# A two-layer attention step on one core: both attentions rewritten from "item after item" to a pipeline in beats

## The chip, the core and the metric

One core of a Trainium2 chip runs the whole program. Five engines work from queues of their own: TensorE (PE, with its weight loads listed as PEld), VectorE (DVE), ScalarE (ACT), GpSimd (POOL), and SyncE (SP), which here only issues DMAs. Each engine takes its instructions in the order in which they stand in its queue, and an instruction that waits holds up everything behind it on that engine. The metric is the device time of one execution in microseconds (us): the median of three runs before is 3446.29 us (3445.15 to 3455.32).

## The reference

2048 prompt frames and 64 sample frames of width 1024 (16 heads of 64) pass through two layers, all in float32:

```
# layer 0 (mixer A)
q, k, v, gate = split(rms_norm(x) @ w_in_a, 4)
s = q @ k.T * 0.125 + rel_bias;  masked to the own chunk of 64 frames and the 8 chunks before it
x = x + ((softmax(s) @ v) * silu(gate)) @ w_out_a
# shared keys and values, from the new x
k, v = split(rms_norm(x) @ w_kv, 2)
# layer 1 (mixer B), strictly causal, over all frames (the sample: 2048 cached frames and its own)
q, gate = split(rms_norm(x) @ w_in_b, 2)
z = q @ k.T * 0.125
w = exp(log_sigmoid(z) + sum over later keys of log_sigmoid(-z))      # stick breaking
x = x + ((w @ v) * silu(gate)) @ w_out_b
y = rms_norm(x)
```

The new k and v rows of both layers are outputs too.

## The kernel before

**Precision.** A float32 operand x is kept as two parts, hi = copy of x in the PE's float32 format and lo = x - hi (`split`: ACT writes hi at L136, DVE subtracts at L137). A projection then takes three matmuls instead of one (L155 to L157).

**Stages.** Four stages follow one another: projections of layer 0, attention A ("band"), projections of layer 1, attention B ("sticks"). Projections go through DRAM: q, k, v and gate are stored per pair of heads (`hp`, 8 pairs) and loaded again by the attentions. The q/k/gate projections of the second half of the frames are partly put off (`DEFER`): k of head pairs 6 and 7 in A, gate and q of all pairs in B. They are done during the attention, as its filler.

**Attention.** Queries are taken in groups of 512 (g = 0 to 3), in the order of `ORDER`: part (1, 0), then part (3, 2); within a part by head pair, then group, then head h. An item of B is one (hp, g, h, c): 4 query tiles of 128 against key chunk c of 512, c from g down to 0. For each tile the PE makes scores z (L465), ACT takes the sigmoid f (L1006), POOL multiplies neighbouring pairs (`two`, L1017), DVE scans the running product over the pairs (L1019; whole rows at L1009 on the diagonal), and POOL fills in the elements between (L1022). The scan starts from the carry of the chunk c+1. An item of A is one (hp, g, h): per tile scores over 640 keys, DVE adds the bias and finds the minimum (L821), ACT takes exp (L826), DVE the reciprocal (L828), POOL scales (L829).

`weigh` then transposes the weights in blocks of up to 4 x 128 columns into a PSUM bank `wt` (PE, L128), splits them into `ph` and `pl` (L136, L137) and multiplies both with v into the bank `acc` (L497). Because B works with differences of neighbouring v rows, each tile of B also needs the last value of its diagonal: a matmul with `last_values` and the selector `upto` adds it (L507; L545 for the sample). `gate_out` sums the two halves of `acc` (ACT L475, DVE L476), multiplies by the gate (POOL L478) and stores.

**The order of the work.** `pipelined` walks through the items with a lag of one item: the four tiles of an item are written out one by one, and behind each one or two of the `weigh` blocks of the item in front, transposes, split and products of a block together. After a block a step of the filler may follow, at a rate worked out for the part. Filler are, in this order: the put-off projections (`ps_j`, L599 to L601; 6 matmuls a step, the weights of a job cut in one step of 8 ACT and 8 DVE instructions), the cut of the output weights (`w_out_steps`: each row's load is followed at once by its split, through the buffers `gt` that the gates use too), two pauses of 10 and 2 steps, and the output projections of the part that is done (`ps_o`, L690 to L692). What is left runs behind the last matmul of the attention (`tc.issue_after`). `LEAD` steps of filler (8 in A, 12 in B) run ahead of the first item.

What the code writes out is not yet the order on the engines: the program is built with `schedule_with_timeline_sim=True`, and a planner hands out the instructions in the order in which its own model of the times finds them ready, what was written first going first. The order of each queue is fixed by this before the program runs.

**Buffers** that matter: z has 2 PSUM banks; `wt` has 3 in A and 4 in B and is also used by the filler's sums; `acc` has 1; `ph` and `pl` 4 each; f 3; the passed rows `s` 9 in A and 11 in B; key and value chunks 4 each in B.

Of the kernel before, what the change touches and what calls it, by code (L numbers as in the profile page):

```python
# [9 lines left out]
F32 = mybir.dt.float32  # L10
# [6 lines left out]
P = 128  # L17
D = 1024
NK = D // P
H = 16  # L20
# [23 lines left out]
LEAD = dict(a=8, b=12)  # L44
LATER = dict(a=(100, 100), b=(150, 0))
# [22 lines left out]

@with_exitstack
def encoder_step(ctx: ExitStack, tc: tile.TileContext, a: dict, o: dict):  # L70
    nc = tc.nc
    mm = nc.tensor.matmul
# [16 lines left out]
    nc.vector.tensor_copy(identr, ident)  # L89
    nhalf = cpool.tile([P, 1], F32, name="nhalf")  # L90
    nc.gpsimd.memset(nhalf, -0.5)
# [20 lines left out]
    vend = dram.tile([len(TOK), H, P], F32R, name="v_end")  # L112

# [13 lines left out]
    def flip(out, in_):  # L127
        nc.tensor.transpose(out, in_, ident[: in_.shape[0], : in_.shape[0]])  # L128

    banks = {}  # L130
    done_late = set()
    last_mm = [None]


    def split(hi, lo, src):
        nc.scalar.activation(hi, src, AF.Copy)  # L136
        nc.vector.tensor_tensor(lo, src, f32(hi), ALU.subtract)  # L137

    def scaled_split(hi, lo, src, g):
        for k in range(NK):  # L140
            nc.scalar.activation(hi[:, k], src[:, k], AF.Copy, scale=g[:, k : k + 1])
            nc.vector.scalar_tensor_tensor(lo[:, k], src[:, k], g[:, k : k + 1], f32(hi[:, k]), ALU.mult, ALU.subtract)

    def rstd_of(pool, xt, n, junk):
        ss = pool.tile([P, 1], F32, name="ss", tag="ss", bufs=4)
        nc.scalar.activation(junk[:n], xt[:n], AF.Square, accum_out=ss[:n])
        ms = pool.tile([P, 1], F32, name="ms", tag="ms", bufs=4)
        nc.vector.tensor_scalar(ms[:n], ss[:n], 1.0 / D, EPS, ALU.mult, ALU.add)
        r = pool.tile([P, 1], F32, name="rstd", tag="rstd", bufs=4)
        nc.gpsimd.tensor_tensor(r[:n], ms[:n], nhalf[:n], ALU.pow)  # L150
# [14 lines left out]
    def projections(L, x_of, begin, w_v, cv, gv, out_v, jobs, first, prompt, sample, stages):  # L165
        with (
# [7 lines left out]
            with tc.tile_pool(name=f"v_{L}", bufs=2) as pool:  # L174

                def normed(t, scale=nc.gpsimd.tensor_scalar):
# [12 lines left out]
                order = [t for gs_ in ORDER for g in gs_ for t in range(4 * g, 4 * g + 4)] + [len(TOK) - 1]  # L189
                if L == "a":  # L190
                    order.sort()
                normed(order[0], nc.vector.tensor_scalar)
                begin()
                for half in range(2):
                    wh, wl = [], []
                    for k in range(NK):
# [5 lines left out]
                        nc.scalar.activation(h_, raw, AF.Copy, scale=gv[:, k : k + 1])  # L202
                        nc.vector.scalar_tensor_tensor(
# [4 lines left out]
                    for i, t in enumerate(order):  # L208
                        r0, n = TOK[t]
                        if half == 0 and i + 1 < len(TOK):  # L210
                            normed(order[i + 1])
# [19 lines left out]
                        if dst is not None:  # L231
                            vn = pool.tile([P, CH], F32, name="vn", tag="vn", bufs=2)
                            nc.scalar.activation(vn[:n], ps[:n], AF.Copy)
# [6 lines left out]
            with tc.tile_pool(name=f"st_{L}", bufs=5) as spool, tc.tile_pool(name=f"t_{L}", bufs=2) as pool:  # L240
                for j, (kind, w, c0, g) in enumerate(jobs):
                    for hp in range(HP):
# [10 lines left out]
                        for hf, (r0, n, chunks) in enumerate(HALVES):  # L253
# [9 lines left out]
                            for c, m in chunks:  # L263
# [8 lines left out]
                                if kind == "g":  # L272
                                    nc.scalar.activation(sg[:, c : c + m], ps[:, :m], AF.Silu)
# [7 lines left out]
                            if kind == "k":  # L281

                                cols = slice(hp * P, hp * P + P)
                                for c in range(0, HALF, CH):
                                    b = hf * HALF + c - first
                                    if b >= 0:
                                        kf = pool.tile([P, CH], F32, name="kf", tag="kf", bufs=2)
                                        part = slice(c, c + CH)
                                        nc.gpsimd.tensor_tensor(kf, f32(sh[:, part]), f32(sl[:, part]), ALU.add)
                                        natural(pool, psum, kf, 0, P, 4, prompt[b : b + CH, cols])  # L290
                                if hf == 0:
                                    kf = pool.tile([P, CH], F32, name="kf", tag="kf", bufs=2)
                                    part = slice(NEW, NEW + NS)
                                    nc.gpsimd.tensor_tensor(kf[:, :NS], f32(sh[:, part]), f32(sl[:, part]), ALU.add)
# [31 lines left out]
    def stage_diff(where, t, half, pool, psum):  # L326
# [5 lines left out]
        if where == "cache":  # L332
# [3 lines left out]
            else:  # L336
                nc.gpsimd.memset(prev, 0.0)
# [10 lines left out]
        nc.gpsimd.tensor_tensor(prev[:n], prev[:n], cur[:n], ALU.subtract)  # L348
# [4 lines left out]

    def stage_ends(half, pool, psum):
        cols, heads, n = slice(half * CH, half * CH + CH), slice(half * 8, half * 8 + 8), len(TOK)
        cur = pool.tile([P, CH], F32, name="vcur", tag="vr", bufs=2)
        nc.sync.dma_start(cur[: n - 1], vraw[1 : 1 + NP, cols].rearrange("(t p) c -> t p c", p=P)[:, P - 1])
        nc.sync.dma_start(cur[n - 1 : n], vraw[T : T + 1, cols])
        vs = pool.tile([P, 8, 2, DH], F32R, name="vs", tag="vs", bufs=2)
        split(vs[:n, :, 0, :], vs[:n, :, 1, :], cur[:n].rearrange("p (h d) -> p h d", d=DH))  # L360
        nc.sync.dma_start(f32(vend[:, heads]), f32(vs[:n]).rearrange("p h s d -> p h (s d)"))
# [799 lines left out]
```

## Time and profile before

| | |
|---|---|
| median of 3 runs | 3446.29 us |
| the profiled execution | 3465.09 us |
| its span, first to last instruction | 3463.4 us |
| granted TensorE clock in it, mean | 0.986 |
| PE busy | 3315.4 us |
| DVE busy | 1937.2 us |
| ACT busy | 1666.5 us |
| POOL busy | 1176.1 us |

The profile's page gives busy time for each engine and for the costliest groups of instructions; other views of the trace give the same for chosen stretches, the waits (who waited for whom), and the chain of work that ended last. The end of a matmul is modelled in it, and matmuls overlap in the rows: the durations of a group of matmuls can add up to more than the time that they took.

### The profile page before, as it was taken

To read this page: it belongs to the slowest core of one execution; us is meant where nothing else is said; L and a number is where in the kernel's file an instruction comes from. 1 tells how busy PE (TensorE), PEld (TensorE's weight loads), DVE (VectorE), ACT (ScalarE), POOL (GpSimd) and SP (SyncE) were. 2 spreads that over 40 slices of the span, in tenths; PEclk is the share of its full clock that TensorE was granted. 3 is DMA by queue.
4 is the path that set the end of the run, shared out by engine and by line. 5 is a ranking of instruction groups with operands and counts; after the bars stand their busy time and mean duration, and the time that the engine had idled before them with its cause. 6 is when DMAs were issued, how large, how long until landed. Compare 5 with 4: busy or idle time off the path is not lost.

```text
span 3463.4 us, 53601 instructions
## 1 busy us (share of the span) xinstructions
PE 3315.4 (96%) x18064; PEld 2829.5 (82%) x18064; DVE 1937.2 (56%) x3863; ACT 1666.5 (48%) x3609; POOL 1176.1 (34%) x1845
## 2 busy tenths in 40 slices
PE   8999999998988999999999998999999999999999
PEld 6789999987877998787899997777777776777777
DVE  3224431127888874221244336777877788777763
ACT  4223322237877773141244335555655566655641
POOL 2002210004443431020233004333466676666650
PEclk9999999999999999999999999999999999999999
DMA  6359983258898974443699568665543465434433
GB/s 187 131 191 367 342 290 132 101 180 235 239 250 239 244 201 158 130 153 107 212 347 347 193 204 223 166 178 160 165 112 98 127 179 144 109 113 135 123 99 112
DMA packets 455776, 642.52 MB, mean 186 GB/s; under 512 B 50009, under 2 KB 269177, under 8 KB 455485
## 3 DMA queue, kind: packets, MB, share of 16 engines
q1 hardware_dynamic: 396046, 587.98, 55.2%
q10 hardware_dynamic: 59456, 51.13, 4.6%
q8 instruction: 143, 2.34, 0.3%
q14 instruction: 131, 1.07, 0.1%
HBM read 387.94 MB, written 251.04 MB: 184 GB/s over the span
## 4 chain that ended last, share of the span: by engine, by line
PE 75%; DVE 10%; DMA 6%; ACT 3%; issue 3%; POOL 1%; SPq 0%; ACTq 0%; DVEq 0%; POOLq 0%
PE ps_t L156 8%; PE ps_t L155 8%; PE ps_t L157 8%; PE acc L497 8%; PE z L465 6%; PE wt L128 6%; PE ps_v L157 4%; PE ps_v L156 4%; PE ps_v L155 4%; PE ps_o L690 3%; PE ps_o L691 3%; PE ps_o L692 3%; DVE pl L137 3%; DVE s L1009 2%; DVE s L1019 2%
## 5 line engine op out<-in xcount | busy, mean ns | idle before, releaser
L128 PE MATMUL wt<-ident,s 128*128 128x128 f32 (+1 forms) x3472 | 561.5, 278 | 34.5 <-DVE pp L137 8.4
L137 DVE TENSOR_TENSOR pl<-wt,ph 128x512 fp32r<-128x512 f32 (+1 forms) x864 | 539.6, 653 | 75.4 <-ACT ph L136 73.2
L128 PEld LDWEIGHTS wt<-ident,s 128*128 128x128 f32 (+1 forms) x3472 | 425.2, 142 | 126.8 <-DVE pl L137 12.8
L136 ACT ACTIVATE ph<-wt 128x512 fp32r<-128x512 f32 (+1 forms) x864 | 464.0, 583 | 128.9 <-PE wt L128 112.1
L1006 ACT ACTIVATE f<-z 128x512 f32<-128x512 f32 (+4 forms) x680 | 354.0, 543 | 312.5 <-PE z L465 156.2
L1022 POOL TENSOR_TENSOR s<-f,s 128x256 f32<-128x256 f32 x416 | 364.8, 878 | 168.4 <-DVE s L1019 162.1
L465 PE MATMUL z<-kt,q 128*128 128x512 f32 (+3 forms) x1280 | 390.2, 400 | 22.9 <-ACT f L1006 13.1
L497 PE MATMUL acc<-pl,vt 128*128 128x512 f32 (+3 forms) x1088 | 370.4, 374 | 33.8 <-DVE pl L137 32.3
L155 PE MATMUL ps_t<-x_own,wh 128*128 128x362 f32 (+1 forms) x1152 | 378.6, 329 | 0.0
L157 PE MATMUL ps_t<-x_own,wl 128*128 128x362 f32 (+1 forms) x1152 | 377.9, 328 | 0.0
L156 PE MATMUL ps_t<-x_own,wh 128*128 128x362 f32 (+1 forms) x1152 | 377.4, 328 | 0.0
L829 POOL TENSOR_SCALAR s<-s,rc 128x640 f32<-128x640 f32 (+5 forms) x264 | 194.5, 744 | 538.3 <-DMA gt<-gate_a 282.8
L497 PE MATMUL acc<-ph,vt 128*128 128x512 f32 (+3 forms) x1088 | 359.2, 364 | 6.2 <-ACT ph L136 3.3
L1019 DVE TENSOR_TENSOR_SCAN s<-two,s,own 128x256 f32<-128x256 f32 x384 | 279.5, 738 | 75.2 <-POOL two L1017 73.7
L1017 POOL TENSOR_TENSOR two<-f 128x256 f32<-128x256 f32 x416 | 259.1, 628 | 125.2 <-ACT f L1006 124.2
L497 PEld LDWEIGHTS acc<-pl,vt 128*128 128x128 f32 x1088 | 196.0, 192 | 83.1 <-DVE pl L137 66.4
L465 PEld LDWEIGHTS z<-kt,q 128*128 128x128 f32 x1280 | 206.3, 194 | 56.5 <-ACT f L1006 32.5
L137 DVE TENSOR_TENSOR sl<-ps_t,sh 128x362 fp32r<-128x362 f32 (+2 forms) x140 | 81.1, 582 | 302.7 <-ACT sh L136 286.6
L497 PEld LDWEIGHTS acc<-ph,vt 128*128 128x128 f32 x1088 | 204.5, 192 | 42.9 <-ACT ph L136 14.6
L1009 DVE TENSOR_TENSOR_SCAN s<-f,own 128x128 f32<-128x128 f32 (+4 forms) x264 | 201.6, 789 | 47.0 <-ACT f L1006 46.0
L156 PEld LDWEIGHTS ps_t<-x_own,wh 128*128 128x128 f32 x1152 | 217.0, 188 | 0.8
L155 PEld LDWEIGHTS ps_t<-x_own,wh 128*128 128x128 f32 x1152 | 216.9, 188 | 0.8
(155 smaller groups left out, 6534.7 us busy)
## 6 DMA issues: line engine op xcount, KB each, us to landing
vt<-v_b SPq DMA_DIRECT2D x80, 512.0 KB, 5.4
v_b<-vs SPq DMA_DIRECT2D x64, 512.0 KB, 6.1
q<-q_a SPq DMA_DIRECT2D x128, 256.0 KB, 4.9
q<-q_b SPq DMA_DIRECT2D x128, 256.0 KB, 4.7
vt<-v_a SPq DMA_DIRECT2D x48, 512.0 KB, 7.5
kt<-k_b SPq DMA_DIRECT2D x96, 256.0 KB, 6.6
keys<-k_a SPq DMA_DIRECT2D x80, 256.0 KB, 6.4
v_a<-vs ACTq DMA_DIRECT2D x32, 512.0 KB, 2.8
```

What stands on the lines that cost most here:

```text
L128: nc.tensor.transpose(out, in_, ident[: in_.shape[0], : in_.shape[0]])
L136: nc.scalar.activation(hi, src, AF.Copy)
L137: nc.vector.tensor_tensor(lo, src, f32(hi), ALU.subtract)
L155: mm(out, sh(k), mh(k), start=(k == 0), stop=False)
L156: mm(out, sh(k), ml(k), start=False, stop=False)
L157: mm(out, sl(k), mh(k), start=False, stop=(k == NK - 1))
L465: mm(z, q[:, i, t * P : t * P + P], kt[:, h], start=(i == 0), stop=(stop and i == 1), skip_group_check=not stop,)
L497: last_mm[0] = mm(acc[:, c0 : c0 + m], v, part[:, at : at + m], start=(first and s == 0 and i == 0), stop=(last and s == 1 and i == len(bl ...
L1006: nc.scalar.activation(f[:, x0:], z, AF.Sigmoid, scale=-SCALE)
L1009: nc.vector.tensor_tensor_scan(pr[:, rev], f[:, rev], own[:, rev], 1.0 if carry_in is None else carry_in, ALU.mult, ALU.max if diag else A ...
L1019: nc.vector.tensor_tensor_scan(pr[:, CH - 2 :: -2], two[:, ::-1], own[:, : CH // 2], carry_in, ALU.mult, ALU.bypass)
L1022: nc.gpsimd.tensor_tensor(pr[:, 1:CH:2], by2[:, :, 1], pr[:, 2 : CH + 1 : 2], ALU.mult)
```

## The change

The diff has 1419 lines. Its parts:

1. **Beats.** `pipelined` is replaced by the class `Beat`. A beat writes out: the next step of each tile that is under way, one step of each list of small leftovers, then scores of one new tile and transposes with split of the blocks that are due (in A the scores first, in B the transposes first), then the products of blocks that were transposed at least `HOLD` beats before (1 in A, 2 in B), then filler. The first block of an item of four tiles is transposed `LAG` beats behind its last tile (2 in A, 5 in B). So a tile of B is spread over four beats: scores and sigmoid; pairs; scan; elements between.
2. **Filler as jobs** of (steps ahead, products, steps behind). The load of a job is issued at the first product of the job in front; its cuts are written in pieces of 2 rows (put-off projections) or halves (output tiles) over the second half of that job's products. Rows of the output weights are loaded three ahead, whole (512 KB instead of 2 x 256 KB), into the buffers `oh` and `ol`; a row counts as half a step. Filler is paced by a fixed number of steps a beat (`RATE`: 0.4 in A, 0.3 in B). Output tiles of a group join the filler when that group's last products are out (`when_summed`). `LEAD` is 8 in both. The rest runs at the end, without `issue_after`.
3. **Last values of B.** The matmuls L507 and L545, `last_values`, `upto`, their preparation and `stage_ends` are gone. One filler job (`end_values`) loads the 17 rows, transposes them with 8 PE transposes and keeps them as a small table; POOL adds them to `ot` in front of the gate.
4. **Sum of the halves in A.** ACT copies both halves of `acc` out (two instructions instead of one) and POOL adds them; before, DVE added. In B and for the sample DVE still adds.
5. **Loads.** Keys are loaded ahead of values, the gate only at the first block of the last item that needs it.
6. **Banks and buffers.** B: `wt` 3 instead of 4, `acc` 2 instead of 1, `ph` and `pl` 5 instead of 4, f 4 instead of 3; the row buffer `s` is taken at the scan instead of at the scores.

A wrapper `InOrder` could pin instructions to the order in which they are written; its switch `on` is set to False throughout, so it does nothing.

```diff
-LEAD = dict(a=8, b=12)
-LATER = dict(a=(100, 100), b=(150, 0))
+RATE = dict(a=0.4, b=0.3)
+LAG = dict(a=2, b=5)
+LEAD = dict(a=8, b=8)
+HOLD = dict(a=1, b=2)
...
-    def gate_out(L, pool, acc, h, c0, n, gt, ot, hp, g):
+    def gate_steps(L, pool, acc, h, c0, n, gt, sums, hp, g):
...
+        def shift():
+            if "ot" not in sums:
+                sums["ot"] = pool.tile([P, CH], F32, name="ot", tag="ot", bufs=2)
+            sums[h] = pool.tile([P, CH], F32, name="otmp", tag="otmp", bufs=1)
+            act.activation(sums[h][mine, :n], acc()[other, c0 : c0 + n], AF.Copy)
+            if L == "a" and n > NS:
+                act.activation(sums["ot"][mine, :n], acc()[mine, c0 : c0 + n], AF.Copy)
+        def close():
+            ot, tmp = sums["ot"], sums.pop(h)
+            if L == "a" and n > NS:
+                gps.tensor_tensor(ot[mine, :n], ot[mine, :n], tmp[mine, :n], ALU.add)
+            else:
+                dve.tensor_tensor(ot[mine, :n], acc()[mine, c0 : c0 + n], tmp[mine, :n], ALU.add)
+            if h == 0:
+                return
+            if L == "b":
+                t0, m = g * (CH // P), max(n // P, 1)
+                by = ot[:, :n].rearrange("p (t q) -> p t q", t=m)
+                last = ends["b"][:, hp, t0 : t0 + m].unsqueeze(2).to_broadcast([P, m, n // m])
+                gps.tensor_tensor(by, by, last, ALU.add)
+            gps.tensor_tensor(ot[:, :n], ot[:, :n], gt()[:, :n], ALU.mult)
             nc.sync.dma_start(lay[L]["o"][g][hp], ot[:, :n])
...
-            if ends and s == 0:
-                mm(acc, *ends, start=False, stop=False, skip_group_check=True)
...
+        def cut(k0):
+            ks = slice(k0, k0 + STEP)
+            scaled_split(st["wh"][:, ks], st["wl"][:, ks], st["raw"][:, ks], g[:, ks])
...
+    def w_out_steps(src, w):
+        def load(k):
+            if k < NK:
+                tag = ("oh", "ol")[k % 2]
+                raws[k] = opool.tile([P, D], F32, name="woraw", tag=tag, bufs=2)
+                nc.sync.dma_start(raws[k], src[k * P : (k + 1) * P])
...
+            ([partial(load, i) for i in range(3)] if k == 0 else [], [None], [[partial(cut, k), partial(load, k + 3)]])
...
+    class Beat:
...
+        def beat(self, first=None):
+            for tile in list(self.tiles):
+                tile.pop(0)()
+            self.tiles = [t for t in self.tiles if t]
+            self.one_rest()
...
+            while self.blocks and self.blocks[0][0] <= self.clock:
+                due.append(self.blocks.pop(0)[1:])
...
+            if first and self.scores_first:
+                self.tiles.append(first())
+            if due:
+                turn()
+            if first and not self.scores_first:
+                self.tiles.append(first())
+            self.products()
+            while due:
+                turn()
+            self.clock += 1
+            self.due = min(self.due + self.rate, 2.0)
+            while (self.now or self.beside) and self.due >= 1.0:
+                cost = self.step()
+                if not cost:
+                    break
+                self.due -= cost
+        def item(self, firsts, blocks):
+            for i, block in enumerate(blocks):
+                self.blocks.append((self.clock + len(firsts) - 1 + self.lag + i * len(firsts) // len(blocks), *block))
+            for first in firsts:
+                self.beat(first)
...
-        banks.update(wt=4, fo="wt")
+        banks.update(wt=3, fo="wt", ph=5)
...
+            def pairs():
+                gps.tensor_tensor(two, by2[:, :, 0], by2[:, :, 1], ALU.mult)
+            def scan():
+                to, carry = pr(), carry_in()
...
+            def between():
+                to, carry = st
+                gps.tensor_copy(to[:, CH : CH + 1], carry)
+                gps.tensor_tensor(to[:, 1:CH:2], by2[:, :, 1], to[:, 2 : CH + 1 : 2], ALU.mult)
...
+            return [pairs, scan, between]
...
+        def acc_bank():
+            return psum.tile([P, CH], F32, name="acc", tag="acc", bufs=2)
```

793 lines of the change are left out of this document (430 added, 363 removed).

## The prediction

> **What bounds the kernel now.** I read the page first, then busy time by stage, then the waits of the two attentions, then the chain of work that ended last, and only then single groups.
>
> ```profile
> PE 3315.4 (96%) x18064; PEld 2829.5 (82%) x18064; DVE 1937.2 (56%) x3863; ACT 1666.5 (48%) x3609; POOL 1176.1 (34%) x1845
> ```
>
> By this line the PE is full and nothing is to be won. The stages say otherwise. The columns are: stretch, its length, then busy time (and instructions) of PE, PEld, DVE, ACT and POOL, granted clock, DMA share, GB/s. The five stretches are projections of layer 0, attention A with the first output tiles, the rest of A's output with the projections of layer 1, attention B, and the output tiles behind B.
>
> ```profile
> 0.00:757.00 757.00, 743.06 (x3833) 656.92 (x3834) 226.90 (x499) 230.68 (x513) 83.30 (x89) 1.00 0.61 211
> 757.00:1342.00 585.00, 545.07 (x3450) 486.10 (x3449) 461.39 (x1240) 431.40 (x970) 242.23 (x310) 0.96 0.83 229
> 1342.00:2093.00 751.00, 742.49 (x3898) 655.97 (x3897) 220.13 (x418) 231.13 (x502) 126.10 (x142) 1.00 0.62 212
> 2093.00:3342.00 1249.00, 1172.86 (x6372) 940.91 (x6371) 981.92 (x1638) 745.99 (x1581) 709.62 (x1283) 0.98 0.50 141
> 3342.00:3463.40 121.40, 111.89 (x518) 89.57 (x516) 46.88 (x71) 27.26 (x47) 14.88 (x22) 0.99 0.34 112
> ```
>
> In the projections the PE is busy 98 to 99%; the change does not touch them, nor the output tiles at the end. What can move lies in A (585 us) and B (1249 us). There the PE shows 39.9 and 76.1 us of idle time, and DVE is at 79% in both (461.4/585 and 981.9/1249).
>
> PE busy hides short stalls, because matmuls overlap in the rows. In a stretch that is nothing but 512-column output matmuls, one starts every 40/178 = 0.225 us, while the row of such a matmul lasts 0.39 us:
>
> ```profile
> 1342.00:1382.00 40.00, 40.00 (x178) 33.13 (x177) 15.21 (x18) 8.18 (x10) 1.69 (x2) 1.00 0.59 190
> ...
> L691 PE MATMUL ps_o<-big,oh 128*128 128x512 f32 (+1 forms) x544 | 214.5, 394 | 0.0
> ```
>
> So after each matmul some 0.17 us of standstill still counts as busy, and the 76 us in B are a lower bound of the PE's loss. The Trainium skill (Perfetto Trace Analysis, Identifying the Most-Contended Engine) states the same of matmul busy time and takes the share of weight loads as the measure. The trace agrees: PEld has 656.0/751 = 87% in the third stage and 940.9/1249 = 75% in B. By that rule B at 87% would take 1077 us; by PE busy it could not go below 1173.
>
> What the PE waits for in B (waiter, releaser, us in total, times, longest):
>
> ```profile
> PEld acc L497 <- DVE pl L137: 61.5, 101, 2.0
> DVE ot L476 <- ACT otmp L475: 55.5, 27, 4.3
> ACT f L1006 <- POOL s L1022: 55.0, 55, 3.3
> ...
> PEld z L465 <- ACT f L1006: 32.5, 74, 5.9
> ...
> PEld wt L128 <- POOL s L1022: 11.8, 20, 1.2
> ...
> PEld acc L497 <- ACT ph L136: 11.1, 44, 1.1
> ACT big L136 <- DMA woraw<-in_w_out_b: 10.8, 10, 3.1
> ```
>
> Many short waits, none of them for an engine that is full: products stand right behind the split of their own block, and scores wait for a z bank whose sigmoid is late. In A there are in addition a few long ones, in the stretch without PE filler around the output weights (950 to 1100 us):
>
> ```profile
> ACT big L136 <- DMA woraw<-in_w_out_a: 18.3, 8, 6.9
> PEld z L465 <- DVE mn L821: 18.1, 14, 8.3
> ...
> ACT oh L136 <- DMA og<-o_a: 8.4, 1, 8.4
> ```
>
> ACT waits up to 6.9 us for a row of weights loaded a moment before; exp and splits queue behind it on ACT, and the PE behind those.
>
> **The change part by part.** Everything is summed against the profiled execution (3465.09 us, span 3463.4); the median of the runs is 18.8 us lower, and I subtract the differences from it. A measurement of this kernel tells about 0.3% (10 us) from no change.
>
> *Output weights loaded three rows ahead, output tiles one job ahead.* In A this takes away the ACT waits of 18.3 and 8.4 us: **-27 us**. That the chain runs through them speaks for taking them whole (shares of A's 585 us, 4.5% is 26 us):
>
> ```profile
> by line: PE acc L497 17.6%; PE wt L128 14.8%; PE z L465 14.7%; issue 4.6%; DMA woraw<-in_w_out_a 4.5%; DMA vt<-v_a 4.3%; DVE pl L137 4.0%; DVE s L821 3.9%; PE ps_o L690 3.4%; PE ps_o L691 3.2%; PE ps_o L692 3.1%; DMA q<-q_a 2.6%; PE acc L53
> ```
>
> The next thing late there is a v load (4.3%, 25 us) that the change only reorders, so I take no more. B's 10.8 us are inside B's term.
>
> *Last values.* 64 matmuls go, and 16 short ones:
>
> ```profile
> L507 PE MATMUL acc<-upto,last_values 128*128 128x512 f32 x64 | 25.6, 400 | 0.0
> L478 POOL TENSOR_TENSOR ot<-ot,gt 128x512 f32<-128x512 f32 x64 | 82.6, 1290 | 143.7 <-DVE ot L476 126.3 <-DMA gt<-gate_a 17.4
> ```
>
> At the pitch of 0.225 us that is 14.4 us of PE. Instead POOL adds over 128x512, once for each head pair and group of B: 32 x 1.29 (the nearest row, L478) = 41 us more on POOL, which is idle 539 of B's 1249 us. The ends: free, or +41 if each one holds up the pairs (L1017) behind it on POOL and with them a scan; I take 0, since scans run beats ahead of their transposes. The new job's 8 transposes and two loads are one filler step.
>
> *Halves summed in A.* For 64 (hp, g, h) DVE loses an addition, ACT gains a copy, POOL gains an addition:
>
> ```profile
> L476 DVE TENSOR_TENSOR ot<-acc,otmp 64x512 f32<-64x512 f32 x128 | 87.7, 685 | 67.3 <-ACT otmp L475 65.5
> L475 ACT ACTIVATE otmp<-acc 64x512 f32<-64x512 f32 x128 | 76.0, 593 | 79.9 <-PE acc L497 77.2
> ```
>
> DVE -44, ACT +38, POOL up to +83 us. A then holds ACT 469, DVE 418, POOL 325 of 558 us. ACT at 84% becomes A's fullest engine; at its best stretch (44.31 of 50 us, quoted below) it reaches 89%, so A could not end below 469/0.886 = 530. Inside 558 I take 0 for this part; between -28 and +38 it could be anything.
>
> *Beats in B.* The four steps of a tile stand a beat apart, transposes 5 beats behind, products 2 beats behind their split; cuts of filler weights come in pieces of 2 instead of 8 pairs. The number of beats follows from the tiles; two stretches show how full DVE and ACT can get when something else does not hold them up:
>
> ```profile
> L1006 ACT ACTIVATE f<-z 128x512 f32<-128x512 f32 (+4 forms) x680 | 354.0, 543 | 312.5 <-PE z L465 156.2
> 800.00:850.00 50.00, 48.82 (x330) 42.75 (x329) 46.94 (x140) 44.31 (x108) 26.91 (x37) 1.00 0.92 243
> 2826.00:2866.00 40.00, 34.60 (x180) 25.83 (x179) 37.12 (x57) 27.41 (x54) 29.52 (x50) 0.96 0.51 145
> ```
>
> 680 tiles in 1249 us are 1.84 us a beat. A split takes about 0.6 us on ACT and 0.65 on DVE, so a hold of two beats (3.7 us) covers it with room for a queue. What the PE no longer waits for, DVE must deliver: its 981.9 us in B stay as they are. The ends for B: nothing gained (79% DVE), or the 93% of the stretch at 2826 us (37.12/40), 981.9/0.928 = 1058. I take 85%, nearer the middle, because the planner fixes each queue by modelled times and some of its errors remain: 981.9/0.85 = 1155, **-94 us**. PE work, 14 us smaller, fits in that.
>
> *Banks.* B falls from 4 `wt` banks to 3, one of them taken by a filler sum. A ran with 3 and the filler all along:
>
> ```profile
> PEld wt L128 <- DVE pl L137: 8.8, 18, 1.6
> ```
>
> That is A's wait for a free bank (585 us); scaled to B, 8.8 x 1249/585 = 19 us. Ends 0 and +19; the 85% contain it. The second `acc` bank in B counts 0: no wait for that bank stands among the long ones above.
>
> *Gates loaded late.* The gate is asked for at the first block of the last item and used some 7 beats (13 us) later; the loads landed in
>
> ```profile
> gt<-gate_a SPq DMA_DIRECT2D x32, 256.0 KB, 7.8
> gt<-gate_b SPq DMA_DIRECT2D x32, 256.0 KB, 3.5
> kt<-k_b SPq DMA_DIRECT2D x96, 256.0 KB, 6.6
> vt<-v_b SPq DMA_DIRECT2D x80, 512.0 KB, 5.4
> ```
>
> so it stays covered: 0. The lead of 8 instead of 12 steps moves 4 steps of filler later, 0. A longer fill and drain of the pipeline costs a few beats once in each attention, inside the terms.
>
> **Sum:** 3446.3 - 27 - 94 = **3325 us**. With B at 82 to 89% and A at -15 to -55 this likeliest case spans 3246 to 3380.
>
> **The rivals.**
>
> *The beats wash out.* The code's order is only a priority for a planner that hands out what its model finds ready; the products could be put right behind their splits again. For it: the switch that would pin the order is off. Against: with a PE queue that always has something else, later-written work does move back. Then only the loads (27 + 10.8) and 14.4 us of PE remain: -52, 3394 us.
>
> *All the slack is used.* DVE at its 93% in B (-191), ACT at 89% in A (-55): 3200 us. For it: no single engine is full in B. (The Trainium skill's rule above would give -172 in B.) Against: 93% was reached only where PE had no filler.
>
> *Values held too long (slower).* In B the products of an item move from beats 4 to 7 behind its start to beats 10 to 13, so each of the 4 v buffers is held 6 beats (11 us) longer. At a change of head in part (3, 2) the first v load finds the last buffer of the old head still in use; SP waits, and behind it stand the keys of the next items. Two beats late plus 6.6 us of landing are 10.3 us, 8 heads make 82 us; against the 52 us of the case above the kernel comes to 3476 us. It decides from 6.5 us a head (52/8). For it: the four buffers did not grow. Against: counted in beats, the values of the new head are needed 4 beats (7.4 us) after the buffer is free and land in 5.4, and a load that is not ready can be planned behind the keys.
>
> *Nothing in sum.* Banks (+19) and additions on POOL (+41) at their bad ends eat the 52: 3446, within 10 us.
>
> **Chances.** Likeliest case 0.42, wash-out 0.22, all slack 0.08, nothing 0.08, values held too long 0.20. Faster by over 0.3% is the first three, 0.72; within it 0.08; slower 0.20. The range from 3225 to 3480 leaves out about half of "all slack" and half of the slower case.
>
> **What would show it.** Right: between the attention's first and last scores B takes about 1155 us with DVE near 85%; the wait of acc (L497) on pl falls from 61.5 us to under 20; ACT's wait for the weight rows is gone from A; POOL's busy time grows by about 41 us in B and 80 in A. Washed out: the wait on pl stays above 45 us. Held values: waits of PE or SP on v or k loads of over 5 us at each change of head. Wrong altogether: DVE's busy time in B grows, or A gets longer because ACT now makes the PE wait.

## The result, and the profile after

| | before | after |
|---|---|---|
| median of 4 runs each, on one chip | 3447.44 us | 3367.57 us |
| ratio, 95% interval | | 0.9766 (0.9748 to 0.9783) |
| the profiled execution | 3465.09 us | 3368.72 us |
| its span / mean granted clock | 3463.4 us / 0.986 | 3366.9 us / 0.992 |

The change makes the kernel faster by 2.3%, about 80 us. Faster was the forecast, by 121 us. The profiled execution of before lies some 18 us above its median, so the two profiles differ by 96.4 us, and what stages lose between them adds up to more than the 80 us. In the kernel after, a wrapper class records most instructions, so they stand under one line, L86; they are told apart by their tiles, and rows that stood under several lines before can stand in one row after.

Page of the kernel after, busy time of each engine:

```profile
PE 3244.7 (96%) x17992; PEld 2800.6 (83%) x17992; DVE 1902.1 (56%) x3807; ACT 1717.3 (51%) x3706; POOL 1277.2 (38%) x1913
```

PE's share is unchanged at 96% in a shorter kernel: once more this row doesn't show what was won. The same five stages as in the prediction (length, then PE, PEld, DVE, ACT, POOL, clock, DMA share, GB/s):

```profile
0.00:756.00 756.00, 742.68 (x3832) 656.60 (x3832) 228.30 (x498) 230.43 (x512) 83.57 (x89) 1.00 0.60 211
756.00:1342.00 586.00, 543.59 (x3475) 487.89 (x3476) 426.81 (x1173) 455.64 (x1025) 321.04 (x367) 0.98 0.83 228
1342.00:2066.00 724.00, 718.98 (x3823) 637.64 (x3821) 213.03 (x423) 234.13 (x516) 119.94 (x110) 1.00 0.63 214
2066.00:3260.00 1194.00, 1140.62 (x6413) 939.35 (x6412) 995.97 (x1652) 775.62 (x1613) 744.74 (x1334) 0.99 0.55 153
3260.00:3366.90 106.90, 98.87 (x455) 79.12 (x453) 37.99 (x63) 21.48 (x43) 7.88 (x13) 0.97 0.32 109
```

Round bounds cut the two kernels at different places of their work. So the stages below are measured between the same landmarks in each trace: the first matmul of a put-off projection (start of A), the first of layer 1's v projection, the last matmul of its q and k projections (into `ps_t`, start of B), the last score, and the end of the last calculation.

| us | A with all its output tiles | projections of layer 1 | attention B, to its last score | B's rest |
|---|---|---|---|---|
| before | 713.4 | 609.0 | 1268.1 | 112.4 |
| after | 706.0 | 604.0 | 1188.0 | 108.9 |
| difference | -7.4 | -5.0 | -80.1 | -3.5 |

How far can single profiles be trusted here? Attention A is the same code in the kernel before and in experiments 5 and 7 below, and takes 713.4, 716.7 and 709.7 us; it is the same in the kernel after and in experiments 1, 2, 3, 4, 6 and 11, and takes 702.9 to 709.0. So A's gain of some 7 us holds in the means (713.3 and 705.9). The -5.0 of the projections does not: they take 605.4 and 604.7 us in experiments 5 and 7, whose code is there that of before. And the 18 us by which the profile of before is long seem to lie mostly in B: the profile of experiment 5, an execution at its median, has 29 us less than before in B with its rest (1351.4 against 1380.5 us), though the medians of the two differ by 10. Against a usual execution of before, the gain of B with its rest is therefore, as an estimate, nearer 65 us than the 83.6 of the table (1351.4 + 10 - 1296.9).

The gain is in attention B. Between its landmarks, first the kernel before, then the one after:

```profile
2079.00:3347.00 1268.00, 1189.54 (x6450) 954.46 (x6449) 991.19 (x1658) 754.91 (x1598) 722.80 (x1324) 0.98 0.51 143
```

```profile
2066.00:3254.00 1188.00, 1135.01 (x6377) 934.74 (x6376) 990.40 (x1644) 771.72 (x1606) 741.00 (x1328) 0.99 0.55 153
```

DVE does the same 990 us of work in less time: 78% busy before, 83% after. PEld rises from 75% to 79%, still below the 88% (637.64/724) of the projections of layer 1. By the measure of the Trainium skill that the prediction cites (Perfetto Trace Analysis, Identifying the Most-Contended Engine) the PE still has headroom in B.

Waits in B after (waiter, releaser: us, times, longest):

```profile
PEld acc L86 <- DVE pl L86: 48.9, 70, 3.1
ACT f L86 <- POOL s L86: 42.2, 47, 3.8
...
PEld z L86 <- ACT f L86: 17.0, 42, 1.2
...
PEld wt L86 <- DVE pl L86: 4.1, 7, 1.0
...
ACT otmp L86 <- PE acc L86: 2.6, 5, 1.0
```

Against the prediction's rows, the wait of products on their split fell only from 61.5 to 48.9 and that of scores on sigmoids from 32.5 to 17.0. The sigmoids' wait on POOL is one row after and was two before, since POOL writes `s` at two lines. Beside the 55.0 us that the prediction quotes stood

```profile
ACT f L1006 <- POOL s L1018: 22.3, 13, 2.6
```

so like is compared with like as 77.3 before and 42.2 after. The row of the copies `otmp`, the last above, had a large counterpart before, which the prediction shows only inside a row for the whole program (77.2 us before the copies `otmp`) and gives no term:

```profile
ACT otmp L475 <- PE acc L497: 67.1, 33, 5.9
```

In the kernel before, the copy out of `acc` stood in ACT's queue while the last products of that bank were still to come, up to 5.9 us, with sigmoids and splits behind it. After, the wait is nearly gone. The copy did not move away from its products: in the code it is still written right behind them (only the addition stands a beat later), and on ACT it starts on average 0.47 us behind the last product, before 0.19. What differs in the code is that these products are written two beats behind their split, and that `acc` has two banks.

In A (756 to 1342 us), the largest DMA waits of ACT were these before:

```profile
ACT big L136 <- DMA woraw<-in_w_out_a: 22.3, 10, 6.9
ACT oh L136 <- DMA og<-o_a: 8.4, 1, 8.4
```

and after, beside two waits of the PE:

```profile
PEld z L86 <- DVE mn L86: 11.7, 25, 1.5
PEld acc L86 <- ACT ot L86: 10.5, 18, 3.6
ACT sp L86 <- DMA k_a<-sp: 9.3, 1, 9.3
ACT ot L86 <- DMA o_a<-ot: 7.9, 3, 3.3
...
ACT oh L86 <- DMA og<-o_a: 5.6, 1, 5.6
```

The wait for weight rows is gone (18.3 of its 22.3 us are the prediction's row). Two that were not there before stand in its place: `k_a<-sp` is ACT waiting until the store of a put-off projection has emptied its buffer, `o_a<-ot` the new copy into `ot` waiting for the store of the one before. A's chain of waits, shares of 586 us, has one of them:

```profile
by line: PE acc L86 18.0%; PE z L86 14.2%; PE wt L86 13.5%; PE ps_o L86 12.1%; ACT s L86 4.0%; issue 3.7%; DMA o_a<-ot 3.3%; DVE pl L86 2.7%; ACT ph L86 2.4%; DVE s L86 1.8%; ACT ot L86 1.7%; ACT otmp L86 1.4%; DMA gt<-gate_a 1.4%; DMA bs<-
```

### The profile page after: what moved, and what is told of

The parts are those of the page before. It is cut to its first block, busy times and chain, and to the rows that moved or that the text cites. A ratio compares the mean times of both kernels' runs of the same rounds, so it can differ in the third digit from the quotient of the medians.

```text
span 3366.9 us, 53591 instructions
## 1 busy us (share of the span) xinstructions
PE 3244.7 (96%) x17992; PEld 2800.6 (83%) x17992; DVE 1902.1 (56%) x3807; ACT 1717.3 (51%) x3706; POOL 1277.2 (38%) x1913
## 4 chain that ended last, share of the span: by engine, by line
PE 58%; DVE 7%; ACT 3%; DMA 3%; issue 3%; POOL 1%; SPq 0%; DVEq 0%; ACTq 0%; POOLq 0%
PE ps_t L86 10%; PE ps_o L86 10%; PE acc L86 10%; PE z L86 8%; PE wt L86 8%; PE ps_v L86 6%; PE ps_j L86 5%; DVE s L86 2%; DVE pl L86 2%; ACT ph L86 1%; ACT s L86 1%; DMA o_a<-ot 1%; POOL s L86 1%; DVE ol L86 1%; DVE lwl L86 1%
## 5 line engine op out<-in xcount | busy, mean ns | idle before, releaser
L86 DVE TENSOR_TENSOR pl<-wt,ph 128x512 fp32r<-128x512 f32 (+1 forms) x864 | 551.4, 653 | 134.6 <-ACT ph L86 131.1
L86 ACT ACTIVATE ph<-wt 128x512 fp32r<-128x512 f32 (+1 forms) x864 | 483.9, 578 | 197.2 <-PE wt L86 179.1
L86 PE MATMUL wt<-ident,s 128*128 128x128 f32 (+1 forms) x3472 | 553.2, 276 | 22.7 <-DVE pl L86 8.2
L86 PE MATMUL ps_t<-x_own,wh 128*128 128x362 f32 (+1 forms) x2304 | 569.9, 328 | 0.0
L86 PEld LDWEIGHTS wt<-ident,s 128*128 128x128 f32 (+1 forms) x3472 | 419.3, 142 | 97.2 <-DVE pl L86 12.6
L86 ACT ACTIVATE f<-z 128x512 f32<-128x512 f32 (+4 forms) x680 | 355.6, 535 | 231.9 <-PE z L86 141.9
L86 POOL TENSOR_TENSOR s<-f,s 128x256 f32<-128x256 f32 x416 | 364.1, 876 | 126.3 <-DVE s L86 113.5
L86 PEld LDWEIGHTS ps_t<-x_own,wh 128*128 128x128 f32 x2304 | 404.5, 188 | 1.9
L86 PE MATMUL acc<-pl,vt 128*128 128x512 f32 (+3 forms) x1088 | 367.9, 372 | 28.6 <-DVE pl L86 27.0
L86 PE MATMUL acc<-ph,vt 128*128 128x512 f32 (+3 forms) x1088 | 375.3, 379 | 17.7 <-ACT ph L86 11.5
L86 PE MATMUL z<-kt,q 128*128 128x512 f32 (+3 forms) x1280 | 375.7, 381 | 9.5 <-ACT f L86 4.7
L86 PE MATMUL ps_t<-x_own,wl 128*128 128x362 f32 (+1 forms) x1152 | 377.2, 327 | 0.0
L86 POOL TENSOR_SCALAR s<-s,rc 128x640 f32<-128x640 f32 (+5 forms) x264 | 196.1, 750 | 477.2 <-DMA keys<-k_a 284.5
L86 PE MATMUL ps_o<-big,oh 128*128 128x512 f32 (+1 forms) x1088 | 342.5, 393 | 5.5 <-ACT oh L86 5.3
L86 POOL TENSOR_TENSOR two<-f 128x256 f32<-128x256 f32 x416 | 265.5, 640 | 163.8 <-ACT f L86 160.4
L86 DVE TENSOR_TENSOR_SCAN s<-two,s,own 128x256 f32<-128x256 f32 x408 | 298.8, 736 | 45.6 <-POOL two L86 39.6
L86 PE MATMUL ps_t<-big,wh 128*128 128x512 f32 x960 | 298.6, 391 | 0.0
L86 PEld LDWEIGHTS z<-kt,q 128*128 128x128 f32 x1280 | 220.1, 191 | 44.3 <-ACT f L86 17.0
L86 PEld LDWEIGHTS acc<-pl,vt 128*128 128x128 f32 x1088 | 196.1, 191 | 70.6 <-DVE pl L86 54.8
L86 DVE TENSOR_TENSOR sl<-ps_t,sh 128x362 fp32r<-128x362 f32 (+2 forms) x140 | 81.3, 582 | 301.5 <-ACT sh L86 284.0
L86 PEld LDWEIGHTS ps_o<-big,oh 128*128 128x128 f32 (+1 forms) x1088 | 198.9, 185 | 50.7 <-ACT oh L86 5.5
L86 PEld LDWEIGHTS acc<-ph,vt 128*128 128x128 f32 x1088 | 199.4, 191 | 44.0 <-ACT ph L86 19.0
```

The costliest lines, as they stand in the source:

```text
L86: ins = op(*args, **kwargs)
```

## The experiments

Each ratio stands against the kernel before on the same chip. The median of before was 3447.4 to 3450.6 us on these chips, so a difference of 3 us between medians of two experiments says nothing. Experiments 1 to 4 vary the written order of B, 5 to 7 the last values and the buffers f, 8 to 11 single parts beside them, and 12 puts the findings together. Stage lengths are between the landmarks above; "B" is there attention B with its rest (1296.9 us after).

**1. Products in the beat of their split** (b_hold0)

```diff
-HOLD = dict(a=1, b=2)
+HOLD = dict(a=1, b=0)
```

> The changed kernel with HOLD 0 instead of 2 in B: products are written in the beat of their own split. Theory 1, the hold gives the split its time: the wait of the products on pl grows from 49.6 us back to 60 us and above, and B gets 30 to 80 us slower (3400 to 3450 us). Theory 2, the planner washes the hold out (in the changed kernel a product starts only 1.4 us behind its split, not two beats): within 12 us of the changed kernel's 3368.

Measured: 3379.36 us, ratio 0.9795 (0.978 to 0.9809), 12 us slower than the kernel after. The intervals of the two ratios just overlap, but each of its four runs is slower than each of the four of the kernel after. The time is that of theory 2, at its edge. Waits in B, of this kernel:

```profile
PEld acc L86 <- DVE pl L86: 53.9, 76, 2.3
...
ACT otmp L86 <- PE acc L86: 17.7, 12, 4.1
...
DVE ot L86 <- ACT otmp L86: 15.8, 19, 2.7
```

The wait that the hold was to remove is nearly the same with it (48.9) and without (53.9). What comes back in part is ACT's wait on the last products of `acc`: without a hold, the products that stand in front of the copy are written in the beat of their split. Averaged over all columns of B, the time from the end of a split on DVE to its matmul is 2.23 us before, 1.42 after, 1.34 here: far from the two beats (3.5 us) that the code writes. The planner pulls the products forward.

**2. The written order kept on the engines, in B alone** (b_pinned)

```diff
-        order.on = False
+        order.on = True
```

> The changed kernel with all of PE, DVE, ACT and POOL held to the written order in attention B. The hold is then real: products two beats behind their splits. Theory 1, the planner's freedom keeps the pipeline from working (wash-out): the wait of acc on pl falls under 20 us and the total under 3355. Theory 2, the freedom is worth more than the hold: slower than 3368 by over 20 us, since a late instruction can no longer be passed.

Measured: 3427.65 us, ratio 0.9946 (0.9931 to 0.9961), 60 us slower than the kernel after; B takes 1349.4 us. Waits in B, of this kernel:

```profile
ACT ph L86 <- PE wt L86: 239.8, 349, 6.7
...
PEld wt L86 <- DVE pl L86: 57.0, 64, 3.2
...
PEld acc L86 <- DVE pl L86: 25.0, 27, 2.3
...
PEld wt L86 <- POOL two L86: 14.4, 13, 2.5
```

Held to the written order, the products do wait less for their split (25.0). But a transposition then waits 57.0 us for one of the three `wt` banks, against 4.1 in the free order. So the planner's freedom as a whole is worth 60 us here, and the pinned order loses most of the gain. All four engines are pinned at once, so this run does not say what the hold alone would cost if it were kept.

**3. and 4. Transposes closer behind their tiles** (b_lag3; b_lag2 has b=2)

```diff
-LAG = dict(a=2, b=5)
+LAG = dict(a=2, b=3)
```

> The changed kernel with LAG 3 in B, the smallest at which an item's transposes are still written behind the last step of its tiles. If a written distance between a tile and its transposes is worth something in spite of the planner: 3385 to 3410, as far as LAG 2 gave (3405). If LAG 2 was slow for another reason: within 10 us of 3368.

> The changed kernel with LAG 2 instead of 5 in B: the first block of an item is transposed 2 beats behind its last tile. Theory 1, the distance between scan and transposes is what B gained: transposes wait for the rows s by tens of us, total 3400 or more. Theory 2, the distance is set by the planner and by buffers: within 12 us of 3368.

Measured: 3382.57 us, ratio 0.981 (0.9795 to 0.9825), and 3404.73 us, ratio 0.986 (0.9844 to 0.9876). At 2 the transposes are written before the last step of the item's last tile, so they do not wait for that step's elements: that kernel leaves out a dependency, and only 3 and 5 compare the same work. Two more beats are worth 15 us by the medians, and 12.7 in B by the profiles (1309.6 against 1296.9). That lies between the two expectations (3385 to 3410, and up to 3378).

**5. The kernel before without its last values** (before_no_ends; this kernel leaves the last-value term out of y)

```diff
-            if ends and s == 0:
-                mm(acc, *ends, start=False, stop=False, skip_group_check=True)
...
-                    if ends and i == 0 and j == 0:
-                        mm(acc[:, h * P : h * P + NS], *ends[h], start=False, stop=False, skip_group_check=True)
```

> The kernel before without the 80 matmuls that add the last values (L507, L545); y of both groups then lacks that term. Their price in the old order: 14 to 16 us if PE's time is what counts there (3447 to 3432), 0 to 5 us if it lies beside the waits of the PE.

Measured: 3437.5 us, ratio 0.9968 (0.9957 to 0.998): the 80 matmuls are worth 10 us, which is between the two prices expected.

**6. Three buffers f instead of four** (b_f3)

```diff
...
-            f = pool.tile([P, CH], F32, name="f", tag="f", bufs=4)
+            f = pool.tile([P, CH], F32, name="f", tag="f", bufs=3)
```

> The changed kernel with 3 buffers f instead of 4 in B. Theory 1, the fourth buffer frees the sigmoid from POOL and so the scores: ACT's wait for POOL s grows from 42 to 55 us and more, the scores' wait for the sigmoid from 17 towards 32 us, total 3390 to 3420. Theory 2, the spacing of the steps does it: within 10 us of 3368.

Measured: 3405.05 us, ratio 0.9877 (0.9856 to 0.9898). As theory 1 expected, one buffer of 2 KB per partition holds 37 us, nearly half of the gain (31.8 of them in B by the profiles, 1328.7 against 1296.9). Two of the waits in B are back near those of before, the products' and the scores'; the sigmoids' wait on POOL is 55.6 us, above the 42.2 of the kernel after and below the 77.3 of before:

```profile
PEld acc L86 <- DVE pl L86: 60.6, 86, 2.5
...
ACT f L86 <- POOL s L86: 55.6, 72, 2.1
...
PEld z L86 <- ACT f L86: 29.6, 66, 2.8
```

ACT cannot write the next sigmoid until POOL's last step has read an old one; then a z bank stays full and the scores wait. As a mean over the 680 tiles of B, with three buffers a tile's scan starts on average 2.11 us behind its sigmoid, with four 2.68, before 1.96.

**7. The fourth f in the old order** (before_ne_f4; leaves the last-value term out of y, as 5 does, with its tables too)

```diff
...
-        last_values = wpool.tile([P, H, P], F32R, name="last_values")
-        upto = wpool.tile([P, T], F32R, name="upto")
...
-            f = pool.tile([P, CH], F32, name="f", tag="f", bufs=3)
+            f = pool.tile([P, CH], F32, name="f", tag="f", bufs=4)
```

> The kernel before without the last values (matmuls, selector and table, as in before_no_ends) and with a fourth buffer f in their place: the buffer alone, in the old written order. Theory 1, the buffer by itself carries its part of the gain: 3437 - 37 = 3400. Theory 2, it pays only together with the new order: within 10 us of 3437.

Measured: 3416.53 us, ratio 0.9911 (0.9895 to 0.9928), 21 us faster than experiment 5 and between the two theories. By the profiles B with its rest is 13.5 us shorter (1351.4 to 1337.9); most of what is left is a shorter A, whose code is the same in both. The buffer stands in the room of the two tables, which take 8 KB and 8.25 KB per partition by their shapes in the code. This run also drops their preparation on POOL, but the first sigmoid of B starts no earlier for it (19.6 us behind the start of B, in experiment 5 18.2). Waits in B, first of experiment 5, then of this one:

```profile
ACT otmp L475 <- PE acc L497: 67.2, 30, 5.8
...
ACT f L1002 <- POOL s L1018: 45.4, 58, 2.6
```

```profile
ACT otmp L475 <- PE acc L497: 60.9, 27, 5.7
...
ACT f L990 <- POOL s L1006: 28.5, 36, 2.3
```

The wait for a free f falls (with the second line of `s` from 67.4 to 39.6 us); the wait of the copies out of `acc` mostly stays. So the buffer pays without the new order too.

**8. Weight rows loaded when they are cut** (wout_late)

```diff
-            ([partial(load, i) for i in range(3)] if k == 0 else [], [None], [[partial(cut, k), partial(load, k + 3)]])
+            ([], [None], [[partial(load, k), partial(cut, k)]])
```

> The changed kernel with each row of output weights loaded in the step that splits it, as before, instead of three rows ahead. If the loads ahead were worth the 27 us in A and 11 in B that I put down to them: 3368 + 30 to 40 = 3400. If ACT's waits for these rows lay beside other waits: +0 to +10.

Measured: 3370.48 us, ratio 0.9767 (0.9753 to 0.9782), the same as after. All that this kernel's waits have on the weight rows, in both attentions:

```profile
ACT big L86 <- DMA woraw<-in_w_out_b: 2.0, 2, 1.6
...
ACT big L86 <- DMA woraw<-in_w_out_a: 0.7, 1, 0.7
```

Loading three rows ahead in the code is worth nothing that can be told: without it ACT hardly waits either. What is left of the change at this place is the buffers (`oh` and `ol` instead of `gt`, which the gates use too) and one DMA for a whole row. Presumably the planner can move the loads ahead once `gt` is left alone; that it is the buffers rather than the row size was not tried apart.

**9. Halves summed by DVE in A too** (a_sum_dve)

```diff
-            if L == "a" and n > NS:
-                act.activation(sums["ot"][mine, :n], acc()[mine, c0 : c0 + n], AF.Copy)
...
-            if L == "a" and n > NS:
-                gps.tensor_tensor(ot[mine, :n], ot[mine, :n], tmp[mine, :n], ALU.add)
-            else:
-                dve.tensor_tensor(ot[mine, :n], acc()[mine, c0 : c0 + n], tmp[mine, :n], ALU.add)
+            dve.tensor_tensor(ot[mine, :n], acc()[mine, c0 : c0 + n], tmp[mine, :n], ALU.add)
```

> The changed kernel with the halves of acc in A summed by DVE as before (ACT copies one half, POOL adds nothing). Theory 1, ACT became A's limit in the part without filler (94% busy there): that part gets shorter, ACT falls by 38 us in A, total 3350 to 3360. Theory 2, A is held by other things: DVE rises by 44 us and the total stays within 8 us of 3368 or gets slower.

Measured: 3366.59 us, ratio 0.975 (0.9735 to 0.9764), the same within what can be told. But the stretch of A without filler differs. The kernel after:

```profile
850.00:900.00 50.00, 45.21 (x315) 41.00 (x314) 41.57 (x129) 47.42 (x115) 37.01 (x45) 1.00 0.88 243
900.00:950.00 50.00, 46.72 (x313) 42.03 (x312) 41.17 (x129) 46.78 (x113) 36.41 (x44) 0.97 0.88 238
```

and with the sum on DVE:

```profile
850.00:900.00 50.00, 48.67 (x330) 43.06 (x329) 47.99 (x147) 46.31 (x109) 28.07 (x39) 1.00 1.00 261
900.00:950.00 50.00, 48.99 (x330) 43.43 (x331) 48.08 (x143) 45.90 (x110) 27.69 (x39) 1.00 0.93 257
```

With the copies ACT is the full engine (47.42 of 50 us) and the PE gets 315 matmuls through; without them 330. A as a whole is 3.6 us shorter (702.4 against 706.0), which is within what profiles of the same A differ by (702.9 to 709.0 us).

**10. The weights of a job cut in one step** (cut_whole)

```diff
-        return [load] + [partial(cut, k0) for k0 in range(0, NK, STEP)], products, behind
+        return [load, lambda: [cut(k0) for k0 in range(0, NK, STEP)]], products, behind
```

> The changed kernel with the weights of a put-off projection cut in one step of 8 pairs of instructions instead of four steps of 2. Theory 1, the bursts on ACT and DVE were a cause of the short stalls in B: total 3380 to 3400. Theory 2, the planner spreads them anyway: within 8 us of 3368.

Measured: 3370.99 us, ratio 0.9788 (0.9768 to 0.9809): no difference that can be told. Cutting in pieces is worth nothing that these runs show.

**11. A fifth f** (f5)

```diff
...
-            f = pool.tile([P, CH], F32, name="f", tag="f", bufs=4)
+            f = pool.tile([P, CH], F32, name="f", tag="f", bufs=5)
```

> The changed kernel with 5 buffers f instead of 4. If what limits B is still how far the sigmoid may run ahead of POOL: another 10 to 30 us off 3368. If four were enough for the four beats of a tile: within 8 us of 3368.

Measured: 3363.49 us, ratio 0.9755 (0.9739 to 0.9771): 4 us faster than after in the medians, inside the intervals. The wait that went from 55.6 to 42.2 us with the fourth buffer goes on falling, and this time the end hardly moves:

```profile
ACT f L86 <- POOL s L86: 18.5, 22, 3.5
```

The row is a poor measure by itself: without the hold (experiment 1), with four buffers, it is 17.0 us in a kernel that is 12 us slower.

**12. The findings together** (combo): five buffers f, A's sum on DVE, and filler spread more evenly: slow through A's first part, and a weight row counted as a whole step in B, where DVE is crowded while rows are cut.

```diff
...
-            return 1.0 if product else 0.5
+            return 1.0 if product else 0.5 if self.scores_first else 1.0
...
+                beat.rate = 0.1 if part == ORDER[0] else RATE["a"]
...
```

> The changed kernel with four edits at once; A and B are told apart by stage. In A: the halves summed on DVE again, and filler paced at 0.1 steps a beat in the part (1, 0) instead of 0.4, so that the put-off projections no longer run out after 57 us. In B: 5 buffers f, and a row of output weights counted as a whole step, so that DVE has twice the beats for their splits. Theory 1, A's expected gain was lost because its filler was spent early: A's segment falls from 706 us to 690 or less. Theory 2, the place of the filler does not matter, since other engines hold A up: A stays within 6 us of 702. In B the stretch of the output weights (21 us idle in 50) gives back some 8 us. Total 3335 to 3350 by theory 1, 3352 to 3364 by theory 2.

Measured: 3354.71 us, ratio 0.9726 (0.9711 to 0.9741), 13 us faster than the kernel after and faster than both kernels. A takes 696.6 us, B 1290.5, with the fifth f alone 1296.4. Both the total and A's length fall within what theory 2 expected (3352 to 3364, and within 6 us of 702), A's barely. A is 5.8 us shorter than with the sum on DVE alone (702.4), about as much as profiles of the same A differ by, and below all of them. So the slower filler in A is worth some 6 us in this pair of profiles, and whether it is worth anything is not settled. In this run the four edits were not tried apart.

## Why the prediction came out as it did

**The sign and B's size: right; the mechanism behind B: wrong.** The forecast for B was 1155 us at 85% of DVE, -94. B took 1188 us between its landmarks at 83.4% (990.40/1188), -80.1 by the two profiles (against a usual execution of before rather less, as estimated above); from its first to its last score, the prediction's own measure, it took 1174 us at 84%, -79. But by its own signs the prediction's likeliest case did not happen. It said that the wait of `acc` on `pl` would fall under 20 us, and that a value above 45 means the beats washed out. It is 48.9, so they did, as experiment 1 confirms; yet the time of that rival (3394 us, in which nothing is gained but the loads and the PE's 14.4 us) is missed by 26 us, because the rival took the hold to be all that B could gain by. The step that failed is "a hold of two beats (3.7 us) covers it": on the engines there is no such hold, the products stand 1.42 us behind their split. That the time still falls into the span of the likeliest case (3246 to 3380) is partly luck: the 85% of DVE was chosen between two ends and did not follow from the hold, and other things filled it. By medians:

| from | to | us | what |
|---|---|---|---|
| before, 3447.4 | without last values, 3437.5 | -10 | PE work dropped |
| 3437.5 | with a fourth f, 3416.5 | -21 | the tables dropped, in their room a buffer: sigmoids wait less for POOL |
| 3416.5 | the kernel after, 3367.6 | -49 | the rest of the change; 41 of it in B by the profiles (1337.9 to 1296.9) |

From the other end: three f cost 37, a lag of 3 costs 15, no hold costs 12. The fourth f is worth more in the new order (37) than in the old (21); why was not tested.

What makes up the 49 us is only partly shown. The lag and hold together are 27 if their effects add, which was not tried. ACT no longer standing in front of unfinished products (67.1 to 2.6 us) is the largest wait that went, and it comes back in part without the hold; that this is how the order gains is argued from these rows, not shown alone. The second `acc` bank, a rival for the same gain, was not tried by itself, nor were the fifth `ph` and `pl` and the pacing of the filler.

**f: not in the sum at all.** The prediction quotes the wait `ACT f <- POOL s` of 55.0 us among the rows of B and lists the fourth buffer in the change, but gives it no term. It was 21 to 37 us of the 80 by the medians (13.5 to 31.8 in B by the profiles).

**Last values: -14.4 us of PE.** Measured -10. The prediction let it vanish inside B's 85% of DVE; taken from the old kernel alone, two thirds of it appear in the time, and the interval leaves 7 to 15 us. The POOL addition was forecast at 32 x 1.29 = 41 us. The groups of the kernel after have 32 of 512 columns and 8 short ones:

```profile
L86 POOL TENSOR_TENSOR ot<-ot,ends 128x512 f32<-128x512 f32 (+1 forms) x40 | 35.9, 898 | 18.4 <-DVE ot L86 18.1 <-DMA kt<-k_b 0.2
```

That is 35.9 us, near enough, and no engine was held up by it that the waits show. As a sign it was less clear: between B's landmarks POOL's busy time grew by only 18.2 us (722.80 to 741.00), since 9.2 us of preparing the dropped tables went (`row` and `upto`, 4.8 and 4.4 us) and some of the additions come behind the last score. In A, POOL's busy time grew by 79 us (242.23 to 321.04), as forecast (80).

**A: -27 forecast, -7.4 measured; this term failed.** The prediction took two waits of ACT whole, 18.3 and 8.4 us. These two kinds of waits did fall between 756 and 1342 us, from 22.3 to 0.3 and from 8.4 to 5.6. But stores that had not held up ACT before now did, for 9.3 and 7.9 us, and all of ACT's waits on DMAs there fell only from 38.9 to 23.1 us. Where the time came back can be seen by pieces: counted as the length of a piece less its matmuls at their closest distance (0.227 us for 512 columns, 0.108 for a transposition), the PE lost 47 us between 950 and 1100 us before and 25 after, a gain of 22 us where the forecast has 27. But it lost 14 us more between 800 and 950 and 5 more behind 1100. The put-off projections are used up at 813 us instead of 952, so the stretch without filler begins earlier, and in it ACT is 94% busy. How much of this is filler spent early and how much ACT stays open (experiment 12).

**Halves in A: taken at 0, between -28 and +38.** Experiment 9 puts the sum at 0 within what can be told. The prediction held ACT to 89% at most; it reaches 95% (47.42/50), and the PE gets 15 matmuls of 330 fewer through.

**Banks: 0 to +19 inside the 85%.** The wait for a `wt` bank is 4.1 us in B, so 0 was right in the planner's order; with B pinned it is 57.0.

**The slower rival** did not occur: PE waits for a key load in B 1.9 us once and for q 2.0 us once; no v load is among its waits.

## What to carry to other kernels

Where a planner fixes the order, a written distance between producer and consumer is only a wish, though not without effect (experiment 3): read the real distance from the trace, and look for what does bind it. Here that was the number of buffers of one tile and, as far as the waits show it, an in-order engine standing before an instruction whose input is not finished. Give every changed buffer count its own term, with the wait whose releaser is the tile's last reader as its upper bound. A wait on one transfer is taken off the path only if the same engine has no other transfer to wait for next.

## What was not expected of the hardware

In these rows POOL's time does not follow the number of partitions: an addition over 64 partitions takes as long as a multiplication over 128, while an addition over 128 whose second operand repeats one value along 128 columns takes a fifth less. The tile's list of the kernel after (duration min/median/max in ns, first and last start in us):

```profile
L86 POOL TENSOR_TENSOR ot<-ot,otmp x64: 1261/1291/1472, 798.9 to 1350.0; 64x512 f32<-64x512 f32 x64
L86 POOL TENSOR_TENSOR ot<-ot,gt x64: 1274/1298/1734, 809.4 to 3266.5; 128x512 f32<-128x512 f32 x64
...
L86 POOL TENSOR_TENSOR ot<-ot,ends x40: 290/1044/1068, 2129.8 to 3278.9; 128x512 f32<-128x512 f32 x32, 128x64 f32<-128x64 f32 x8
```

Where the PE does less, the clock that it is granted is lower. The kernel before and the kernel after, each in the 50 us of A with the fewest matmuls:

```profile
1000.00:1050.00 50.00, 38.61 (x241) 36.63 (x241) 37.15 (x91) 36.44 (x78) 17.42 (x22) 0.83 0.88 240
```

```profile
800.00:850.00 50.00, 43.10 (x260) 37.18 (x258) 42.66 (x108) 43.13 (x98) 29.35 (x33) 0.93 0.85 254
```

The quoted stretches of A with 313 to 330 matmuls have 0.97 to 1.00. The count alone does not set it: the kernel after has 0.97 from 1000 to 1050 us with 265. The Trainium skill (TensorE: Matmul & The Clock Gate, Part 1) describes a clock that drops when the PE has been idle for some microseconds, and these rows agree in direction. What that adds to a stall was not measured.
